# A planned attention stage: other times for its transfers, another spread of the projection products, and an order pinned into the convolution

## The chip, the cores and the metric

The kernel runs on one core of a Trainium2 chip. The metric is the device time of one execution in microseconds (us). The core has five engines with a queue of instructions each: TensorE (PE, with its weight loads listed as PEld), VectorE (DVE), ScalarE (ACT), GpSimd (POOL) and SyncE (SP), which here only issues DMAs.

## The reference

One layer of an encoder on 1024 tokens of width 1024, all in float32. A normed and modulated input goes through one projection whose columns feed a state-space group (SSD) and an attention group; their outputs are projected and added; a convolutional FFN and a final norm follow. Cut to what matters here:

```python
mod = (c_act @ w_ada[l] + b_ada[l])[:, None, :]          # six rows of 1024: shifts, scales, gates
h = rmsnorm(x, norm_mix_w[l]) * (1 + sc_m) + sh_m
z, xbc, dt_raw, q, k, v = jnp.split(h @ w_in[l], IN_SPLITS, axis=-1)
y_ssd = ssd_mixer(z, xbc, dt_raw, ...)   # begins with silu(causal_dwconv(xbc, conv_w) + conv_b), width 4
y_att = chunk_attention(q, k, v, rel_bias[l])   # 8 heads x 64, own chunk of 64 and the 8 before it
x = x + g_m * (jnp.concatenate([y_ssd, y_att], axis=-1) @ w_out[l])
h = rmsnorm(x, norm_ffn_w[l]) * (1 + sc_f) + sh_f
x = x + g_f * conv_ffn(h, w_up[l], ffn_conv_w[l], w_down[l])
return rmsnorm(x, final_norm_w)
```

## The kernel before

Every large product is made of three: both operands are split into a high part (fp32r) and the rest, and high x high, low x high and high x low are added in PSUM (`mm3`, lines 299 to 302). The stages follow each other on the one core: norm and first projection, attention (about 88 to 283 us of the trace), convolution and SSD with the output projection, FFN up, FFN down. The change lies in the attention and the start of the convolution.

**The attention** works on four pairs of heads p, eight query blocks i of 128 rows, and the two heads h of a pair. Each step has a letter: S scores (PE, into a PSUM tile `s`), X adds the bias table and takes the row maximum (DVE, into `p`), E exponential (ACT), R reciprocal of the row sum (DVE), N scaling (POOL), T transposition of a bank of probabilities (PE, into `tp`), H and L the split of that bank into `pt` (ACT copies the high half, DVE subtracts), W the product with the values (PE, into `pv`), C and Y the copy of half of it and its addition into `ya` (ACT, DVE). There is one `pv` bank, so the next W waits until Y has read the last one. B loads a bias table (issued by SP, for pair 0 by ACT) and M masks its corners (two memsets on POOL).

Into the gaps of this chain go the **projection products** F: sixteen groups of 24 products of 512 columns for the pairs 2 and 3, and for blocks 4 and 6 of the convolution's input (p = 4 and 5 in the plan). Their weights come by ld (DMA), wh (ACT, high half) and wl (POOL, low half). The high halves have two buffers in turn, and so do the low halves. Seven more steps, mload and m, load 512 KB of W_ada and take the row sums with the activated condition on DVE; each fills one column of `modc`.

**What sets the order.** `attention_plan` lists all these steps with an engine, a length in ns, what they depend on, a priority, and for transfers the earliest time `at` and how long they take. `Plan.run` places them one after the other, as a simulation with one clock for each engine would, and gives back their names by start time. The instructions are then issued in that order, and `InOrder` pins the order on each of PE, DVE, ACT and POOL: every instruction is tied behind the one before it on its engine. The transfers themselves are not pinned: their times in the table only decide where the steps that use them stand, and a scheduler orders the SP queue. A pinned engine waits at a step whose transfer is late, with everything behind it. `FP` (line 137) gives the priority of the n-th projection product by linear pieces, and with it how the 384 products are spread. `WIDE` stretches the lengths on DVE and ACT. With `slack`, a step that is ready within so many ns may be taken before the earliest one, by priority. The plan walks a Python set, so equal steps can fall differently from one build to the next; the orders shown below are of one build whose order on PE is the one in the trace of before.

Behind the plan, `e.on = False` ends the pinning, and the scheduler alone orders the **convolution**. `conv_silu(ft, dst)` makes one block: weights by `wu_pair` (DMA, ACT high, DVE low), 48 products (`gemm_ft`), an ACT scaling, three DVE multiply-adds, two ACT Silu. Block 4 takes its products from the rows that the plan left, block 6 from a PSUM tile `s` that the plan filled; blocks 5, 7 and 0 to 3 make their own. The code's order is 4, 6, 5, 7. `conv_mods` makes three more row sums behind each block.

Of the kernel before, what the change touches and what calls it, by code (L numbers as in the profile page):

```python
# [17 lines left out]
D = 1024  # L18
# [47 lines left out]
class Plan:  # L66


    TAIL = {"PE": 210, "V": 140, "A": 140, "G": 160, "D": 50}
    WIDE = 1.02  # L70
    OVER = {"PE": 0, "V": 80, "A": 100, "G": 60}

    def __init__(self, start, slack):
# [7 lines left out]
    def add(self, name, eng, ns, deps=(), prio=0, ring=None, until=None, result=0, at=0):  # L81
        self.tasks[name] = (eng, ns * self.WIDE if eng in "VA" else ns, tuple(deps), prio, ring, until, result, at)

# [50 lines left out]

CH2 = [(0, 0), (1, 0), (0, 1), (1, 1), (2, 0), (2, 1)]
CH3 = [(0, 0), (0, 1), (1, 0), (2, 0), (1, 1), (2, 1)]
FP = [(0, 0), (53, 4.04), (137, 7.71), (230, 9.78), (266, 11.49), (323, 14.11), (384, 24.63)]


def weighted_banks(u):  # L140
# [12 lines left out]
    return banks  # L153


def attention_plan(start=88300, slack=30, ahead=(1.14, 0.4)):
    pl = Plan({"PE": start, "V": start, "A": start, "G": start - 3000}, slack)
    for name, n in (("s", 2), ("p", 8), ("tp", 2), ("pt", 3), ("pv", 1), ("acc", 1), ("wh", 2)):
        pl.ring(name, n)
# [2 lines left out]
    V = {128: 300, 256: 420, 384: 560, 512: 690, 640: 810}  # L162
    A = {128: 410, 256: 510, 384: 620, 512: 730, 640: 830}
    G = {128: 380, 256: 480, 384: 580, 512: 690, 640: 800}
# [3 lines left out]
    def fprio(n):  # L168
        for (n0, s0), (n1, s1) in zip(FP, FP[1:]):
            if n <= n1:  # L170
                return s0 + (s1 - s0) * (n - n0) / (n1 - n0)
# [3 lines left out]
    for n, c in enumerate(chain):  # L175
        p, which, hh = c
        for j in range(24):
            deps = [prev] if prev else []
# [30 lines left out]
    for n, (p, which) in enumerate(ws):  # L209
        rel = ("FE", p, which, 1)  # L210
        deps = [("wl",) + ws[n - 2]] if n > 1 else []
        if n > 0:
            deps.append(("wh",) + ws[n - 1])
        at = 88000
# [5 lines left out]
    for p in range(4):  # L220
        for h in range(2):
            n = 2 * p + h
            if p:
                deps = [("X", (n - 3) // 2, 7, (n - 3) % 2)] if n >= 3 else []
                pl.add(("B", p, h), "D", 3600, deps, at=95000)
                pl.add(("M", p, h), "G", 330, [("B", p, h)], 4 * p)
            else:
                pl.add(("B", p, h), "D", 0, at=91800)
                pl.add(("M", p, h), "G", 330, [("B", p, h)], 4 * p)
        for i in range(8):  # L230
            n = 128 * min(i + 1, 5)
            u = 4 * p + i // 2
            for h in range(2):
                deps = []
                if p >= 2:
                    deps = [("MV", p, 0, 0), ("MV", p, 1, 0)]
                    if i > 3:
                        deps += [("MV", p, 0, 1), ("MV", p, 1, 1)]
                if (p, i) != (0, 0):
                    pl.add(("S", p, i, h), "PE", 2 * (n + 32) / 2.4 if n <= 512 else 587, deps,  # L240
                       u - ahead[0] + .1 * (i % 2) + .01 * h, "s", ("X", p, i, h),
                       at=(88000 if i < 4 else 91000) if p == 0 else 98000 if p == 1 else 0)
                else:
                    pl.add(("S", p, i, h), "D", 0, [], 0, "s", ("X", p, i, h))
                pl.add(("X", p, i, h), "V", V[n], [("S", p, i, h)] + ([("M", p, h)] if (p or i > 2) else [])
                       + ([("FA", p, 2, i // 4)] if p > 1 and i in (2, 6) else []),
                       u - ahead[1] + .1 * (i % 2) + .01 * h, "p", ("PF", p, i, h))
                pl.add(("E", p, i, h), "A", A[n], [("X", p, i, h)], u - ahead[1] + .1 * (i % 2) + .01 * h, result=100)
                pl.add(("R", p, i, h), "V", 150, [("E", p, i, h)], u - 2)
                pl.add(("N", p, i, h), "G", G[n], [("R", p, i, h)], u)  # L250
        for u in range(4):
            i0, i1 = 2 * u, 2 * u + 1
            banks = weighted_banks(u)
            for h in range(2):
                pr = 4 * p + u + .03 * h
                for t, bank in enumerate(banks):
                    w = sum(b[2] for b in bank)
                    a = (p, u, h, t)
                    deps = [("N", p, i0, h), ("N", p, i1, h)]
                    deps += turn  # L260
                    if p > 1 and u in (0, 2) and h + t == 0:
                        deps.append(("VT", p, 2, u // 2))
                    turn = [("T",) + a]
                    last = t == len(banks) - 1
                    pl.add(("T",) + a, "PE", w / 128 * 92.5, deps, pr + .01 * t, "tp", ("L",) + a)
                    pl.add(("H",) + a, "A", H[w], [("T",) + a], pr + .01 * t, "pt", ("W",) + a)
                    pl.add(("L",) + a, "V", L[w], [("H",) + a], pr + .01 * t)
                    deps = [("L",) + a] + ([("W", p, u, h, t - 1)] if t else [])
                    if p >= 2:
                        deps.append(("VL", p, 2, 0))  # L270
                        if u > 1:
                            deps.append(("VL", p, 2, 1))
                    pl.add(("W",) + a, "PE", sum(2 * (b[2] + 32) / 2.4 for b in bank), deps, pr + .01 * t - .005,
                           "pv" if t == 0 else None, ("Y", p, u, h))
                pl.add(("C", p, u, h), "A", 390, [("W",) + a], pr - .1)
                pl.add(("Y", p, u, h), "V", 410, [("C", p, u, h)], pr - .1)
                for i in (i0, i1):
                    pl.add(("PF", p, i, h), "D", 0, [("T",) + a])

    for n in range(7):  # L280
        deps = [("m", n - 2)] if n in (2, 3) else [("X", 2, 7, 0), ("X", 2, 7, 1)] if n > 3 else []
        pl.add(("mload", n), "D", 6000 if n < 4 else 5000, deps, at=92000)
        pl.add(("m", n), "V", 1220, [("mload", n)], 90)
    return pl

# [4 lines left out]
def tile_block(ctx: ExitStack, tc: tile.TileContext, x, ccol, pk, w_ada, w_first, w_ft, w_z,  # L290
               w_out, w_up, w_down, bias, fnw, xt, out, dbg=None):
    nc = tc.nc
    V, A, T, G = (InOrder(tc, e) for e in (nc.vector, nc.scalar, nc.tensor, nc.gpsimd))
# [79 lines left out]
    def wu_pair(src, hieng, loeng):  # L373
        t = raw_tile()
        nc.sync.dma_start(t, src)
        wh = wu.tile([P, 1024], F32R, tag="wh", name="wh")
        if not wls:
            wls.append(wu.tile([P, 2, 1024], F32R, tag="w2", bufs=1, name="wl"))
        wl = wls[0][:, rawc[0] % 2, :]
        split(wh, wl, t, hieng, loeng)  # L380
        return wh, wl
# [306 lines left out]
    for hh in range(2):  # L688
# [13 lines left out]
        for kt in range(KT):  # L702
            if hh == 0:
                if kt == 0:
                    bm = mods_first()
                else:
                    at = last_lo.ins if kt == 1 else bm.ins
# [164 lines left out]
    def conv_silu(ft, dst):  # L872
        if ft == 4:
            ps = rowb
        else:
            if ft == 6:
                ps = early["s"]
            else:
                wh, wl = wu_pair(w_ft[ft], A, V)
                ps = s_tile()  # L880
                gemm_ft(wh, wl, [ps[:, 0:512], ps[:, 512:1024]])
        w = [pkt[:, SCW + 4 * ft + j:SCW + 4 * ft + j + 1] for j in range(4)]
        A.activation(dst, ps, AF.Identity, scale=w[3], bias=pkt[:, SCB + ft:SCB + ft + 1])
        for j in range(1, 4):
            last = V.scalar_tensor_tensor(dst[:, j:S], ps[:, 0:S - j], w[3 - j], dst[:, j:S],
                                          op0=ALU.mult, op1=ALU.add)
        for hh in range(2):
            c = slice(hh * 512, hh * 512 + 512)
            sil[:] = [A.activation(dst[:, c], dst[:, c], AF.Silu).ins, last.ins]
        return last.ins  # L890
# [157 lines left out]
    for k in attention_plan().run():  # L1048
        if k[0] in ops:
            ops[k[0]](*k[1:])  # L1050
    for e in (T, V, A, G):
        e.on = False
    es_at.close()


# [33 lines left out]
    def conv_mods(n, at):  # L1089
        for _ in range(CMODS[n]):  # L1090
            k = wosc[0]
            wosc[0] += 1
            t = xs[:, 2 * (k % 4):2 * (k % 4) + 2, :].rearrange("p a b -> p (a b)") if n < 5 else wos[:, k % 3, :]
            mod_col(todo.pop(0), t, at)
# [8 lines left out]
    conv_mods(0, last_v[0])  # L1103
    for g in range(2):
        conv_mods(2 * g + 1, conv_silu(4 + g, bt_[g]))
        if g == 1:
            V.tensor_tensor(gcol[:, 0:8], modc[:, G_M:G_M + 8], gbias[0], ALU.add)
            cols_to_dram(gcol[:, 0:8], tp_tile()[0:8, 0:P], th512()[0:8, 0:P], gmd)
            for t, k in ((rowb[:, 0:512], 0), (gm1, 4)):
                nc.sync.dma_start(t.rearrange("p (a b) -> p a b", a=4), rows_from(gmd, k, 4))  # L1110
        conv_mods(2 * g + 2, conv_silu(6 + g, ct_[g]))
# [394 lines left out]
    at = None  # L1506
    for c in range(NT):
# [5 lines left out]
        if c == 1:  # L1513
            at = wout_rhs(0, 1)
# [6 lines left out]
        n, k = ((0, slice(0, 3)), (2, slice(0, 4)), (3, slice(0, 3)))[c] if c < 3 else (c + 1, slice(0, 3))  # L1521
# [715 lines left out]
```

## Time and profile before

| what | value |
|---|---|
| median of 3 runs | 1163.94 us (1162.77 to 1166.97) |
| profiled execution | 1162.48 us, its span 1160.8 us |
| granted TensorE clock | 0.998 |
| PE, PEld busy | 1143.3 us (98%), 971.4 us (84%) |
| DVE, ACT, POOL busy | 79%, 51%, 13% of the span |
| DMA | 170.72 MB, mean 147 GB/s |

The span runs from the first to the last instruction of the profiled execution; times in the views count from its start. The prediction's rows come from the list of waits (who waited for whom: total, times, longest), from busy times by stretch, and from the timeline of one engine. A row of the timeline has the start and the duration in us, the engine, the line of the kernel, the operation with what it writes and reads, the shapes and, in brackets, the idle time of the engine before it with the instruction that ended it. Line 60 is the helper of `InOrder`, so all pinned instructions carry it; they are told apart by their tiles. A matmul's end is modelled, and successive ones overlap. Rows that follow each other are merged (x8).

### The profile page before, as it was taken

How to read it: one execution, taken by the hardware profiler on the slowest of the kernel's cores; microseconds unless marked ns; L12 is line 12 of the kernel's file. 1: busy time of each engine (PE TensorE's matmuls, PEld its weight loads, DVE VectorE, ACT ScalarE, POOL GpSimd, SP SyncE). 2: the span in 40 equal slices, each digit the busy share in tenths (PEclk: the TensorE clock that was granted, in tenths of full speed). 3: DMA queues.
4: the chain of work that ended last, by engine and by line, in shares of the span. 5: the costliest groups of instructions: out<-in, count | busy, mean ns of one | idle time of the engine just before them, and what ended most of it. 6: DMA issues, size and time to landing. Idle time of an engine off the chain costs nothing.

```text
span 1160.8 us, 15796 instructions
## 1 busy us (share of the span) xinstructions
PE 1143.3 (98%) x5833; PEld 971.4 (84%) x5833; DVE 913.4 (79%) x1365; ACT 592.6 (51%) x987; POOL 149.7 (13%) x180
## 2 busy tenths in 40 slices
PE   9998999999999999999999999999999999999997
PEld 8887988887889988887788888888888888888886
DVE  7857765676875788469999998889888869666987
ACT  5746665564345765576543445334533444433445
POOL 1104333230000455100000000000000000000522
PEclk9999999999999999999999999999999999999999
DMA  9967323335466532231223322332223378633444
GB/s 333 368 168 207 70 68 96 108 109 182 148 215 238 219 109 74 87 113 55 109 84 134 136 82 82 109 136 82 85 106 118 121 288 301 241 119 126 155 145 155
DMA packets 68189, 170.72 MB, mean 147 GB/s; under 512 B 6976, under 2 KB 11792, under 8 KB 66704
## 3 DMA queue, kind: packets, MB, share of 16 engines
q1 hardware_dynamic: 60624, 144.42, 37.4%
q10 hardware_dynamic: 7488, 25.30, 5.5%
q8 instruction: 46, 0.75, 0.3%
q14 instruction: 31, 0.25, 0.1%
HBM read 127.44 MB, written 32.81 MB: 138 GB/s over the span
## 4 chain that ended last, share of the span: by engine, by line
PE 84%; DVE 10%; DMA 2%; ACT 1%; issue 1%; SPq 0%; POOL 0%; POOLq 0%; DVEq 0%; ACTq 0%
PE acc L60 6%; PE wops L1256 5%; PE dn L302 5%; PE dn L301 5%; PE dn L300 5%; PE uY L302 5%; PE uY L301 5%; PE uY L300 5%; PE s L60 4%; PE uX L302 3%; PE uZ L301 3%; PE uZ L300 3%; PE uZ L302 3%; PE uX L301 3%; PE uX L300 3%; PE pv L60 2%
## 5 line engine op out<-in xcount | busy, mean ns | idle before, releaser
L301 PE MATMUL dn<-w 128*128 128x512 f32 x292 | 105.9, 389 | 0.4 <-DVE w L311 0.4
L300 PE MATMUL dn<-w 128*128 128x512 f32 x292 | 105.8, 389 | 0.0
L302 PE MATMUL dn<-w 128*128 128x512 f32 x292 | 98.1, 389 | 0.0
L302 PE MATMUL uY<-tH,w 128*128 128x512 f32 x248 | 96.5, 389 | 0.0
L300 PE MATMUL uY<-tH,w 128*128 128x512 f32 x248 | 96.5, 389 | 0.0
L301 PE MATMUL uY<-tL,w 128*128 128x512 f32 x248 | 96.5, 389 | 0.0
L2027 POOL TENSOR_TENSOR ya<-ya,xs 128x512 f32<-128x512 f32 x4 | 14.7, 3692 | 551.0 <-ACT xs L2023 551.0
L310 ACT ACTIVATE w<-ya 128x1024 fp32r<-128x1024 f32 (+1 forms) x41 | 39.1, 954 | 85.2 <-PE uY L302 75.2
L1256 PE MATMUL wops<-hH,yhl 128*128 128x512 f32 x224 | 72.8, 397 | 0.6 <-DVE yhl L311 0.6
L301 PEld LDWEIGHTS dn<-w 128*128 128x128 f32 x292 | 54.8, 188 | 12.2 <-DVE w L311 0.8
L302 PEld LDWEIGHTS dn<-w 128*128 128x128 f32 x292 | 54.7, 188 | 11.8 <-DVE w L311 0.4
L300 PEld LDWEIGHTS dn<-w 128*128 128x128 f32 x292 | 54.8, 188 | 11.3
L60 POOL TENSOR_SCALAR p<-p,st 128x640 f32<-128x640 f32 (+4 forms) x64 | 43.5, 686 | 119.1 <-DVE st L60 96.0
L310 ACT ACTIVATE w<-xs 128x1024 fp32r<-128x1024 f32 (+1 forms) x41 | 39.1, 954 | 37.0 <-PE uY L302 31.1
L300 PEld LDWEIGHTS uY<-tH,w 128*128 128x128 f32 x248 | 46.6, 188 | 9.7
L302 PEld LDWEIGHTS uY<-tH,w 128*128 128x128 f32 x248 | 46.5, 188 | 9.7
L301 PEld LDWEIGHTS uY<-tL,w 128*128 128x128 f32 x248 | 46.5, 188 | 9.6
L60 DVE CUSTOM_DVE_ANT_0 p<-s,bias 128x640 f32<-128x640 f32 (+4 forms) x58 | 38.1, 674 | 19.0 <-PE s L60 17.0
L1679 DVE SCALAR_TENSOR_TENSOR a<-cv,pkt,a 128x1023 f32<-128x1023 f32 (+1 forms) x40 | 51.0, 1277 | 0.1
L60 ACT ACTIVATE p<-p,st 128x640 f32<-128x640 f32 (+4 forms) x64 | 44.1, 692 | 13.3 <-DVE st L60 13.1
L60 DVE TENSOR_TENSOR pt<-tp,pt 128x512 fp32r<-128x512 f32 (+2 forms) x72 | 41.8, 595 | 11.1 <-ACT pt L60 10.6
L1679 DVE SCALAR_TENSOR_TENSOR a<-cg,pkt,a 128x1023 f32<-128x1023 f32 (+1 forms) x40 | 49.7, 1278 | 0.0
(527 smaller groups left out, 3332.7 us busy)
## 6 DMA issues: line engine op xcount, KB each, us to landing
gz<-a ACTq DMA_DIRECT2D x10, 1024.0 KB, 5.1
ya<-in_w_up_dram SPq DMA_DIRECT2D x11, 768.0 KB, 4.1
xs<-in_w_up_dram SPq DMA_DIRECT2D x11, 768.0 KB, 4.3
adat<-in_w_ada_dram SPq DMA_DIRECT2D x14, 512.0 KB, 5.3
raws<-in_w_ft_dram SPq DMA_DIRECT2D x14, 512.0 KB, 3.6
qk<-qk SPq DMA_DIRECT2D x56, 128.0 KB, 2.4
xs<-in_w_ada_dram SPq DMA_DIRECT2D x12, 512.0 KB, 4.7
gy<-a ACTq DMA_DIRECT2D x10, 512.0 KB, 2.6
```

What stands on the lines that cost most here:

```text
L60: i = op(*a, **k)
L300: T.matmul(ps, lh, rh, start=start, stop=False, skip_group_check=more)
L301: T.matmul(ps, lh, rl, start=False, stop=False, skip_group_check=more)
L302: T.matmul(ps, ll, rh, start=False, stop=stop, skip_group_check=more)
L310: i = A.activation(hi, src, AF.Copy) if ehi is A else ehi.tensor_copy(hi, src)
L1256: i = op(*a, **k)
L1679: V.scalar_tensor_tensor(a[:, j:S], c[:, 0:S - j], w[2 - j], a[:, j:S], op0=ALU.mult, op1=ALU.add)
L2027: G.tensor_tensor(src, src, fnr[:, halves[1]], ALU.mult)
```

## The change

Four things change. The plan's times of transfers: the bias tables of pair 0 at 92.0 and 93.9 us instead of both at 91.8, the first four loads of W_ada from 98.5 us and 8 or 7 us long instead of from 92.0 and 6, the other three 9 us long instead of 5. The planner's settings: lengths on DVE and ACT stretched by 1.04 instead of 1.02, and no slack instead of 30 ns. The knots of `FP`. And where the pinning ends: for POOL behind the plan as before, for DVE and ACT behind block 4 of the convolution with its three row sums, for PE behind the products of block 5.

```diff
-    WIDE = 1.02
+    WIDE = 1.04
...
-FP = [(0, 0), (53, 4.04), (137, 7.71), (230, 9.78), (266, 11.49), (323, 14.11), (384, 24.63)]
+FP = [(0, 0), (53, 3.74), (138, 7.31), (228, 10.09), (270, 10.64), (324, 14.74), (384, 23.55)]
...
-def attention_plan(start=88300, slack=30, ahead=(1.14, 0.4)):
+def attention_plan(start=88300, slack=0, ahead=(1.14, 0.4)):
...
-                pl.add(("B", p, h), "D", 0, at=91800)
+                pl.add(("B", p, h), "D", 0, at=92000 + 1900 * h)
...
-        pl.add(("mload", n), "D", 6000 if n < 4 else 5000, deps, at=92000)
+        pl.add(("mload", n), "D", 8000 if n < 2 else 7000 if n < 4 else 9000, deps, at=98500)
         pl.add(("m", n), "V", 1220, [("mload", n)], 90)
...
     for k in attention_plan().run():
         if k[0] in ops:
             ops[k[0]](*k[1:])
-    for e in (T, V, A, G):
-        e.on = False
+    G.on = False
     es_at.close()
...
     for g in range(2):
         conv_mods(2 * g + 1, conv_silu(4 + g, bt_[g]))
+        for e in (T,) if g else (V, A):
+            e.on = False
```

DVE at the first row sum m(0) of W_ada, before. `ISA ya,modc` is the sum over a load that lies in `ya`, `ISA p` an X with its bias table, `pt<-tp,pt` an L, `ya<-pv,tl` a Y, RECIPROCAL an R:

```order
L60 RECIPROCAL st_72<-st_72 128x1
L60 TENSOR_TENSOR pt<-tp,pt 128x512
L60 TENSOR_TENSOR ya<-pv,tl 64x2x128
L60 TENSOR_TENSOR pt<-tp,pt 128x384
L60 RECIPROCAL st_72<-st_72 128x1
L60 ISA ya,modc<-ya,rows 128x8x128
L60 ISA modc 128x1
L60 RECIPROCAL st_72<-st_72 128x1
L60 TENSOR_TENSOR pt<-tp,pt 128x512
L60 TENSOR_TENSOR ya<-pv,tl 64x2x128
```

DVE at the same sum now:

```order
L60 TENSOR_TENSOR pt<-tp,pt 128x384
L60 ISA p,st_72<-s,bias 128x640
L60 ISA st_72 128x1
L60 RECIPROCAL st_72<-st_72 128x1
L60 ISA p,st_72<-s,bias 128x640
L60 ISA st_72 128x1
L60 TENSOR_TENSOR pt<-tp,pt 128x512
L60 TENSOR_TENSOR ya<-pv,tl 64x2x128
L60 TENSOR_TENSOR pt<-tp,pt 128x512
L60 ISA ya,modc<-ya,rows 128x8x128
L60 ISA modc 128x1
```

The sum has moved 16 places down DVE's queue, from between query blocks 5 and 6 to behind block 7 of pair 0 and the first two subtractions of the third pair of blocks.

DVE at the first of the three late sums, whose loads lie in `qk`, before:

```order
L60 TENSOR_TENSOR pt<-tp,pt 128x512 x2
L60 RECIPROCAL st_72<-st_72 128x1
L60 ISA p,st_72<-s,bias 128x640
L60 ISA st_72 128x1
L60 RECIPROCAL st_72<-st_72 128x1 x2
L60 TENSOR_TENSOR pt<-tp,pt 128x256
L60 TENSOR_TENSOR pt<-tp,pt 128x512
L60 ISA qk,modc<-qk,rows 128x1024
L60 ISA modc 128x1
L60 TENSOR_TENSOR ya<-pv,tl 64x2x128
```

And now:

```order
L60 TENSOR_TENSOR pt<-tp,pt 128x256
L60 TENSOR_TENSOR ya<-pv,tl 64x2x128
L60 ISA p,st_72<-s,bias 128x128
L60 ISA st_72 128x1
L60 ISA p,st_72<-s,bias 128x128
L60 ISA st_72 128x1
L60 ISA p,st_72<-s,bias 128x256
L60 ISA st_72 128x1
L60 TENSOR_TENSOR pt<-tp,pt 128x512 x2
L60 RECIPROCAL st_72<-st_72 128x1 x2
L60 ISA qk,modc<-qk,rows 128x1024
L60 ISA modc 128x1
```

It has moved from right behind pair 2's last bias addition and two subtractions to behind the first three bias additions of pair 3.

PE at the end of block 6's products, which the plan places, before (`s_2852` is block 6's tile, `wh` and `wl_948` the two halves of the weights, `s_3126` block 7's tile):

```order
L60 MATMUL s_2852<-hH1_85,wl_948 128x512
L60 MATMUL s_2852<-hH1_85,wh_2615 128x512
L60 MATMUL s_2852<-hL1_87,wh_2615 128x512
L60 MATMUL s_2852<-hH1_85,wl_948 128x512
L300 MATMUL s_3126<-hH0_84,wh_3123 128x512
L301 MATMUL s_3126<-hL0_86,wh_3123 128x512
L302 MATMUL s_3126<-hH0_84,wl_948 128x512
```

PE there now (`s_2877` is block 6's tile, `s_3053` block 5's):

```order
L60 MATMUL s_2877<-hH1_85,wl_948 128x512
L60 MATMUL s_2877<-hH1_85,wh_2611 128x512
L60 MATMUL s_2877<-hL1_87,wh_2611 128x512
L60 MATMUL s_2877<-hH1_85,wl_948 128x512
L60 MATMUL s_3053<-hH0_84,wh_3050 128x512
L60 MATMUL s_3053<-hL0_86,wh_3050 128x512
L60 MATMUL s_3053<-hH0_84,wl_948 128x512
```

The 48 products of block 5 stood before among the attention's last transpositions and weighted products, ahead of this place; now all of them stand behind block 6's, and block 7 follows them. On SP the bias table of pair 1 now stands ahead of the first two loads of W_ada, which stood before and behind a move of pair 1's keys.

## The prediction, as put on record

> **What bounds the kernel now.** I read the page's busy line first (busy time, share of the span, instructions).
>
> ```profile
> PE 1143.3 (98%) x5833; PEld 971.4 (84%) x5833; DVE 913.4 (79%) x1365; ACT 592.6 (51%) x987; POOL 149.7 (13%) x180
> ```
>
> TensorE (PE) has work for 98% of the span. No instruction of arithmetic goes away in this change, so all that it can win is PE's idle time: 1160.8 - 1143.3 = 17.5 us. The list of waits of PE says which part of that lies where the change works (total, times, longest):
>
> ```profile
> PE pv L60 <- DVE ya L60: 3.8, 2, 2.1
> PE s L302 <- DVE wl L311: 0.9, 1, 0.9
> PE tp L60 <- DVE st L60: 0.9, 1, 0.9
> ```
>
> All four waits are in the attention and at the start of the convolution. Busy time by stretch (PE, PEld, DVE, ACT, POOL, then granted clock, DMA share, GB/s) places three of them: PE is whole in most stretches (20.00) and short in three.
>
> ```profile
> 88.00:100.00 12.00, 11.14 (x68) 9.36 (x67) 9.44 (x39) 9.37 (x27) 5.48 (x13) 1.00 0.89 232
> 100.00:120.00 20.00, 17.94 (x122) 16.17 (x120) 16.63 (x46) 12.51 (x30) 7.96 (x14) 1.00 0.61 166
> 120.00:140.00 20.00, 20.00 (x137) 18.42 (x137) 15.71 (x45) 15.21 (x38) 6.47 (x9) 1.00 0.28 60
> 180.00:200.00 20.00, 20.00 (x118) 17.83 (x118) 11.26 (x29) 10.72 (x23) 6.36 (x6) 1.00 0.33 81
> 200.00:220.00 20.00, 18.26 (x119) 16.11 (x118) 11.82 (x35) 9.65 (x26) 4.23 (x9) 1.00 0.39 122
> ```
>
> The timeline of PE shows the four holes (start, duration, what; in brackets the idle time and who ended it):
>
> ```profile
> 92.54 0.49 PE L60 MATMUL tp<-ident,p 128*128 128x128 f32 x3
> 93.11 0.27 PE L60 MATMUL tp<-ident,p 128*128 128x128 f32 x1
> 94.24 0.44 PE L60 MATMUL tp<-ident,p 128*128 128x128 f32 x2 [0.86 <-DVE st L60]
> 103.23 1.34 PE L60 MATMUL s<-qk 128*128 128x320 f32 x8
> 106.63 1.15 PE L60 MATMUL pv<-pt,v 128*128 128x256 f32 x8 [2.06 <-DVE ya L60]
> 209.00 0.40 PE L60 MATMUL acc<-hH,wl 128*128 128x512 f32 x1
> 211.14 0.75 PE L60 MATMUL pv<-pt,v 128*128 128x256 f32 x4 [1.74 <-DVE ya L60]
> 283.56 0.39 PE L300 MATMUL s<-hH,wh 128*128 128x512 f32 x1
> 283.78 0.39 PE L301 MATMUL s<-hL,wh 128*128 128x512 f32 x1
> 285.11 0.50 PE L302 MATMUL s<-hH,wl 128*128 128x512 f32 x1 [0.94 <-DVE wl L311]
> ```
>
> Products overlap, so the idle time in brackets understates a hole. I measure from start to start and take off what the row before needs when nothing is late. A 512-column product needs 0.227 (283.56 to 283.78), though it is shown as 0.39: its end overlaps the next by 0.16. A transposition needs 0.11 (three in 0.49, one in 0.27), the eight products at 103.23 need 1.34 - 0.16 = 1.18. The holes are 1.13 - 0.11 = **1.02**, 3.40 - 1.18 = **2.22**, 2.14 - 0.23 = **1.91** and 1.33 - 0.23 = **1.10**: together **6.25 us**.
>
> Whether loading weights says the same: PEld's busy time falls to 16.17 between 100 and 120 against 18.42 in the next stretch (2.25 less), and to 16.11 between 200 and 220 against 17.83 before (1.72 less). [...]
>
> **The change part by part.**
>
> *Loads of W_ada (holes 2 and 3).* DVE stands in a pinned order, and a row sum m waits there for its load:
>
> ```profile
> 104.36 1.23 DVE L60 CUSTOM_DVE_ANT_0 ya<-ya,rows 128x1024 f32<-128x1024 f32 x1 [2.73 <-DMA ya<-in_w_ada_dram]
> 111.77 1.28 DVE L60 TENSOR_TENSOR pt<-tp,pt 128x512 fp32r<-128x512 f32 x2
> 200.68 0.80 DVE L60 CUSTOM_DVE_ANT_0 p<-s,bias 128x640 f32<-128x640 f32 x1
> 209.52 1.23 DVE L60 CUSTOM_DVE_ANT_0 qk<-qk,rows 128x1024 f32<-128x1024 f32 x1 [2.73 <-DMA qk<-in_w_ada_dram]
> ```
>
> The addition ya that frees PE's only pv bank is queued behind m (in the order above, the fourth row after the first m): that is how 2.73 us of DVE become 2.22 and 1.91 of PE. The table had counted on the first load at 92.0 + 6.0 = 98.0; it came at 104.36. Now it counts on 98.5 + 8.0 = 106.5. The late three were counted at 5.0 after the last bias addition of pair 2; that ended at 200.68 + 0.80 = 201.48 and the sum began 8.04 later; now 9.0 are allowed. Both allowances exceed what was traced, by 2.1 and 1.0. On DVE m(0) now stands behind the two subtractions that began at 111.77. They ended at 113.05; less the two holes before them (3.24), and less another row sum (1.23) that no longer stands ahead, m(0) comes due at 108.6 to 109.8. The issues decide when the loads land:
>
> ```profile
> 96.37 0.65 SPq L1034 DMA_DIRECT2D ya<-in_w_ada_dram  x1
> 97.13 1.25 SPq L455 DMA_DIRECT2D qk<-qk  x1
> 98.43 0.59 SPq L1034 DMA_DIRECT2D ya<-in_w_ada_dram  x1
> 99.12 0.86 SPq L958 DMA_DIRECT2D bias<-in_bias_dram  x1
> 202.57 1.29 SPq L1037 DMA_DIRECT2D qk<-in_w_ada_dram  x3
> ```
>
> Now the bias table of pair 1 goes first, in the place of 96.37, and both loads follow the move at 97.13, at about 98.4 and 99.0. From the second issue to the sum it took 104.36 - 98.43 = 5.9, so 104.9: 3.7 ahead of need. I take off both holes whole, **-4.1**. Kept for the range: none of it, should a load still be late.
>
> *The first two bias tables (hole 1) and the one of pair 1.* POOL works in a pinned order too (the last row is PE's):
>
> ```profile
> 91.67 0.34 POOL L60 MEMSET bias<- 64x64 f32 x2
> 93.27 0.34 POOL L60 MEMSET bias<- 64x64 f32 x2 [1.25 <-DMA qk<-qk]
> 93.71 1.60 POOL L60 TENSOR_SCALAR p<-p,st 128x256 f32<-128x256 f32 x3
> 98.38 0.80 POOL L60 TENSOR_SCALAR p<-p,st 128x640 f32<-128x640 f32 x1 [0.36 <-PE tp L60]
> 105.19 0.34 POOL L60 MEMSET bias<- 64x64 f32 x2 [6.01 <-DMA bias<-in_bias_dram]
> 109.53 1.03 PE L60 MATMUL tp<-ident,p 128*128 128x128 f32 x8
> ```
>
> The scaling that the transposition at 94.24 needs (the first of the three from 93.71; DVE, which the trace names there, had been done) is queued behind the memset at 93.27, which waits for the second table. With 92.0 and 93.9 in place of twice 91.8 the scaling stands ahead of it: **-1.0**. The price lies at the third memset: it now stands ahead of the scalings of blocks 4, and they wait for its table. Issued at 96.4 instead of 99.12, with the 6.07 that it took before (105.19 - 99.12), that table lands at 102.4; memset 0.34 and three scalings of 0.80 end at 105.2. The first transposition that needs the third is the one at 109.53; less the two holes ahead of it (3.24) it comes due at 106.3. The margin is 1.1 us, so a new wait of 0 to 2: I take **+0.3**.
>
> *The end of the attention (hole 4).* DVE writes the low half of the next weights only after the last product that reads the same half:
>
> ```profile
> 283.82 2.36 DVE L311 TENSOR_TENSOR wl<-raws,wh 128x1024 fp32r<-128x1024 f32 x2 [5.26 <-PE s L60]
> 272.92 0.39 PE L60 MATMUL s<-hL,wh 128*128 128x512 f32 x1
> 273.40 0.33 PE L60 MATMUL tp<-ident,p 128*128 128x128 f32 x1
> 271.33 0.58 ACT L60 ACTIVATE pt<-tp 128x512 fp32r<-128x512 f32 x1
> ```
>
> Before, the 48 products of block 5 had been spent inside the attention, and the block that follows needs this half at once. With PE pinned, they stand behind the last product of block 6: 48 x 0.227 = 10.9 us of cover for 1.2 us of DVE. **-1.1**. DVE and ACT now do no convolution between the attention's last halves, so the small hole at 272.92 (0.48 - 0.23 = 0.25) should close: **-0.25**. The pinning costs that filler: between a transposition and its weighted product lie an ACT copy (0.58), a DVE subtraction (0.64) and handovers, about 1.7. In the new order 1.6 to 2.5 us of other PE rows stand there, so **+0.2**, with bounds of 0 and, with no cover for ten banks, 17.
>
> *At nothing:* slack 0, the cushion 1.04 and the new spread change only places. PE changes its kind of work 253 times instead of 255 in this part, so the gaps at each change stay.
>
> Sum: -1.0 - 4.1 - 1.1 - 0.25 + 0.3 + 0.2 = **-5.95**, say -6.0. The profiled execution took 1162.48 (span 1160.8, 1.7 around it), so 1156.5; the median of the runs is 1.46 higher, 1163.94, and I forecast **1157.9**. What follows stands in the same order on every engine, so the gain should be carried to the end.
>
> **Rivals.**
>
> *A: a transfer still decides.* More bytes now stand ahead of the first loads:
>
> ```profile
> ya<-in_w_ada_dram SPq DMA_DIRECT2D x4, 512.0 KB, 4.2
> bias<-in_bias_dram SPq DMA_DIRECT2D x6, 320.0 KB, 4.6
> ```
>
> With weights, table, move, both loads and the next weights sharing, 2.5 MB at the 232 GB/s of the stretch end at 95.7 + 10.8 = 106.5; or the memset holds POOL 2 us longer. One such wait of 2 to 3 us comes back: gain 2 to 5, about 1160.4. For it: margins of 1.0 and 1.1; against it: those of 2.1 and 3.7. Chance 0.22. [...]
>
> *B: slower, the uncovered tail.* If ACT or DVE lags, each of the ten last banks shows its chain of 1.7: +17 with no cover. It turns the gain into a loss once more than 6 us show, that is when the cover per bank averages below 1.1. At 0.5 per bank: +12 - 6 = +6, 1170. Against it: the order keeps 1.6 or more. Chance 0.06.
>
> *C: the change doesn't do what it says.* The times in the table only order instructions; if PE waits for another engine at the same places, nothing comes of it: 1163.9. DVE's 79% speak against it. Chance 0.04.
>
> *D: more.* The added waits stay out and the wider cushion shortens some of the gaps at PE's changes of work too: gain 7.5 to 9, about 1155.7. Chance 0.06.
>
> **How the numbers follow.** The forecast, a gain of 5.0 to 7.5, has 0.62. A measurement of this kernel can tell about 0.5% from no change, here 5.8 us: 0.44 of the 0.62 lie beyond it and 0.18 within. Faster 0.44 + 0.06 = 0.50; same 0.18 + 0.22 + 0.04 = 0.44; slower 0.06. The range 1155.0 to 1161.5 leaves out B, C and the far ends of A and D.
>
> **What would show it.** In the profile after: the two waits of pv for ya and the one of s for wl gone from PE's list; DVE's sums m without a DMA behind them; PE whole between 100 and 120 and between 200 and 220; block 5's products behind block 6's. Wrong if POOL waits long for a bias table with PE behind it, if PE waits for pt or ya after 240, or if the attention ends less than 4 us earlier.

## The result, and the profile after

The changed kernel takes 1154.31 us (median of 5 runs, 1153.49 to 1155.25) against 1163.89 for the kernel before (5 runs, 1162.77 to 1166.97): ratio 0.9915, interval 0.9900 to 0.9931. It is 9.6 us faster where 6.0 were forecast, and 0.7 below the lower end of the range. The profiled execution took 1154.31, its span is 1152.6: 8.2 less than before.

PE's list of waits after the change (first and last rows):

```profile
PE warm L60 <- POOL mhalf L352: 1.6, 1, 1.6
PE xps L60 <- ACT ya L60: 0.9, 1, 0.9
PE uX L302 <- DVE w L311: 0.6, 1, 0.6
...
PE vps L60 <- DVE hL L544: 0.2, 1, 0.2
```

None of the four waits named in the prediction is left; what is left lies outside the attention. The busy times by stretch, in the columns of before:

```profile
88.00:100.00 12.00, 12.00 (x73) 10.65 (x72) 9.79 (x38) 9.26 (x28) 4.78 (x12) 1.00 0.88 238
100.00:120.00 20.00, 20.00 (x140) 18.55 (x140) 18.13 (x51) 15.00 (x38) 8.80 (x17) 1.00 0.73 179
200.00:220.00 20.00, 20.00 (x125) 17.70 (x124) 13.01 (x35) 10.24 (x26) 7.07 (x7) 1.00 0.43 128
```

PE is whole in all three, and loading weights rose from 16.17 to 18.55 and from 16.11 to 17.70. At the place of the largest hole (PE, start and duration) the scores are now followed without a break, and on DVE the first sum of either group begins with nothing in brackets, so it waits for no transfer:

```profile
103.84 1.33 PE L60 MATMUL s<-qk 128*128 128x320 f32 x8
105.01 0.39 PE L60 MATMUL acc<-hL,wh 128*128 128x512 f32 x1
```
```profile
108.83 1.22 DVE L60 CUSTOM_DVE_ANT_0 ya<-ya,rows 128x1024 f32<-128x1024 f32 x1
208.24 1.20 DVE L60 CUSTOM_DVE_ANT_0 qk<-qk,rows 128x1024 f32<-128x1024 f32 x1
267.35 1.23 DVE L311 TENSOR_TENSOR wl<-raws,wh 128x1024 fp32r<-128x1024 f32 x1 [0.49 <-ACT wh L310]
```

The last row is the low half of the next weights: it is written at 267.35, while block 5's products run, and PE does not wait for it.

POOL around the bias tables of pair 0 and pair 1:

```profile
93.24 0.35 POOL L60 MEMSET bias<- 64x64 f32 x2 [0.25 <-DMA bias<-in_bias_dram]
93.68 0.59 POOL L60 TENSOR_SCALAR p<-p,st 128x384 f32<-128x384 f32 x1
...
100.81 0.35 POOL L60 MEMSET bias<- 64x64 f32 x2 [2.13 <-PE s L60]
101.26 3.93 POOL L60 TENSOR_SCALAR p<-p,st 128x640 f32<-128x640 f32 x5
```

Pair 1's table was issued at 95.90 and its memset ran at 100.81, 4.9 later and not the 6.07 of the forecast; five scalings follow at once and PE waits for none of them.

All holes of PE over 0.11 us from 87 to 345, measured from start to start, were 6.96 in sum before and are 0.35 now. The part as a whole is 7.5 shorter, so gaps under 0.11 us lost another 0.9; 0.7 went outside this part (0.2 ahead of it, 0.5 behind).

One thing must be known for the numbers below. The planner walks through a Python set, and candidates that are equal to it (two loads with the same time, say) come out in an order that differs from one build to the next. The changed program that ran is of another build than the one listed above; the rows shown are the same in both. The kernel before, built anew for the experiments, took 1159.34 to 1159.76 and not 1163.89. So all experiments carry a fixed rank for equal candidates, and are compared with d_before and d_after, which have the traced orders. By the intervals of the ratios a median carries about 1.0 to 1.6 us.

### The profile page after: what moved, and what is told of

It reads as the page before. It is cut to its first block, busy times and chain, and to the rows that moved or that the text cites. A ratio compares the mean times of both kernels' runs of the same rounds, so it can differ in the third digit from the quotient of the medians.

```text
span 1152.6 us, 15803 instructions
## 1 busy us (share of the span) xinstructions
PE 1141.3 (99%) x5833; PEld 971.8 (84%) x5833; DVE 913.7 (79%) x1365; ACT 592.6 (51%) x987; POOL 156.1 (14%) x180
## 4 chain that ended last, share of the span: by engine, by line
PE 89%; DVE 7%; ACT 1%; DMA 1%; issue 1%; POOL 0%; POOLq 0%; DVEq 0%; ACTq 0%
PE acc L60 8%; PE wops L1257 6%; PE dn L302 6%; PE dn L300 6%; PE dn L301 6%; PE s L60 5%; PE uY L302 5%; PE uY L301 5%; PE uY L300 5%; PE uX L302 3%; PE uZ L301 3%; PE uZ L302 3%; PE uZ L300 3%; PE uX L301 3%; PE uX L300 3%; PE pv L60 3%
## 5 line engine op out<-in xcount | busy, mean ns | idle before, releaser
L302 PE MATMUL dn<-w 128*128 128x512 f32 x292 | 98.3, 390 | 0.0
L302 PE MATMUL uY<-tH,w 128*128 128x512 f32 x248 | 96.5, 389 | 0.0
L2028 POOL TENSOR_TENSOR ya<-ya,xs 128x512 f32<-128x512 f32 x4 | 18.2, 4588 | 551.1 <-ACT xs L2024 551.1
L302 PEld LDWEIGHTS dn<-w 128*128 128x128 f32 x292 | 54.7, 188 | 12.1 <-DVE w L311 0.8
L60 POOL TENSOR_SCALAR p<-p,st 128x640 f32<-128x640 f32 (+4 forms) x64 | 46.5, 734 | 116.4 <-DVE st L60 104.1
L302 PEld LDWEIGHTS uY<-tH,w 128*128 128x128 f32 x248 | 46.5, 188 | 9.6
L1257 PEld LDWEIGHTS wops<-hH,yhl 128*128 128x128 f32 x224 | 41.9, 188 | 9.5 <-DVE yhl L311 1.3
```

What stands on the lines that cost most here:

```text
L60: i = op(*a, **k)
L302: T.matmul(ps, ll, rh, start=False, stop=stop, skip_group_check=more)
L1257: i = op(*a, **k)
L2028: G.tensor_tensor(src, src, fnr[:, halves[1]], ALU.mult)
```

## The experiments

**A first try at the rank.** The edit, in the planner (shown with the rank that d_before has; c_before, c_sums and c_pin have "10" in place of "437", and c_after takes the reverse of the order in which the steps are listed):

```
+        def tie(k):
+            return hashlib.md5(("437" + repr(k)).encode()).digest()
-            for k in open_:
+            for k in sorted(open_, key=tie):
```

Four kernels had ranks that gave TensorE's order of the traced kernels, but turned round the two weight loads (2,2) and (3,0), and here and there other equal steps. The low halves of the two weights take each other's buffer, so these kernels compute other projections than the reference.

> The kernel before, with one thing added: equal candidates of the planner are taken by a fixed rank, chosen so that TensorE's order is that of the traced kernel before. Theory (the traced program stands for the kernel, and its profiled execution of 1162.48 lay 1.4 below the median because waits for transfers vary from run to run): ratio 1.000, that is 1163 to 1165; the four holes of 1.0, 2.2, 1.9 and 1.1 us on TensorE again; runs spread over 2 us or more. Rival (the runs of before differ because its builds differ in order): runs within 1 us of each other, at a median more than 1 us away from that of before.

Measured 1169.54.

> The changed kernel with the same kind of fixed rank, chosen so that TensorE's order is that of the traced changed kernel. Theory: ratio 0.991 to 0.992, 1154 to 1155, runs within 2 us since no wait for a transfer is left on TensorE. Rival (part of the gain is a lucky build): 1156 to 1158.

Measured 1161.05. The row that carries it, from c_after's waits of PE:

```profile
PE acc L60 <- POOL wl L60: 4.2, 2, 2.1
```

Neither expectation can be judged: the turned loads alone add waits for the low half of the weights. The two others, c_sums (1162.09) and c_pin (1167.59), were run with the same fault:

> Before in its traced order, with nothing but the seven row sums of W_ada put later in that order (the first four 8 places or more, the late three 2 or more), and of the loads only the third and fourth, which can only follow the first and second sum. Theory (the sums stood ahead of their transfers): holes 2 and 3 go, 4.1 us; the planner's own costs show 0.5 to 0.7 us of new idle time at 118 to 122, where VectorE is full; gain 3.4 to 3.6, about 1160.4, ratio 0.997; holes 1 and 4 stay at 1.0 and 1.1. Rival (the wait of VectorE only passes on to what is queued behind, and the other spread of the products is what removed it): gain under 1.

> Before in its traced order, with nothing but the pinned order carried on into the convolution. The prediction's terms: hole 4, 1.1, and the small hole of 0.25 go, 0.2 comes back: gain 1.15, 1162.8, ratio 0.999. Theory after the result (all three small holes behind 272 go, 0.69, and nothing comes back): gain 1.8 to 2.3, 1161.6 to 1162.1, ratio 0.998. Rival (the uncovered tail): slower by 2 or more.

They are taken up again below with a rank that keeps the order of these loads. What they leave is a price: c_after took 6.2 us more than d_after (1154.88, below). Its trace has two new holes on PE, both in this wait and of 2.26 each, and behind one of them the granted clock was 0.50 (136.99 to 140.40; the last section has the rows). Its rank turns round row sums too, but no hole stands at them.

**The traced orders.** d_before and d_after: the same edit with the rank "437" and "36".

> The kernel before with a fixed rank for equal candidates, chosen so that the order on all engines, that of the weight loads, of the bias tables and of the loads of W_ada included, is that of the traced kernel before. Theory (the order decides the time, the chip and the build otherwise don't): 1163 to 1165 and the four holes of 1.0, 2.2, 1.9 and 1.1 us on TensorE, wherever the kernel before, built anew, comes out. Rival (this chip is faster): at the time of the kernel before as built here, 1159 to 1160.

> The changed kernel with such a rank, in the order of the traced changed kernel on all engines. Theory: 1154 to 1155, 9 to 10 below the one before in its traced order. Rival (this chip is faster): 1150 to 1151.

1164.01 and 1154.88, beside 1159.34 for the kernel before built anew on that chip. The theory holds: the order makes the time, not the chip. The profiled execution of d_before is one of 1164.22, and shows what the trace of before (1162.48) did not. PE at hole 2, then the busy times by stretch (the first of the last three columns is the granted clock):

```profile
108.16 1.16 PE L60 MATMUL pv<-pt,v 128*128 128x256 f32 x8 [2.97 <-DVE ya L60]
...
109.79 2.33 PE L60 MATMUL s<-qk 128*128 128x320 f32 x8
```
```profile
108.00:109.40 1.40, 1.24 (x9) 1.24 (x10) 1.40 (x5) 0.06 (x1) 1.40 (x2) 1.00 0.31 90
109.40:112.10 2.70, 2.70 (x11) 2.56 (x10) 2.64 (x8) 2.05 (x5) 0.17 (x2) 0.52 0.49 148
```

The hole is 3.1 here instead of 2.2, and behind it the granted clock is 0.52 for a while: the eight products with 320 columns take 2.33 instead of 1.33, and with their neighbours about 1.2 us go. Hole 1 is 1.6 instead of 1.0, hole 3 only 1.0. These waits end with transfers and differ from run to run.

**One part alone on before.** The steps of the plan are moved by hand:

```
+    steps = attention_plan().run()
+    for k, anchor in (...):
+        steps.remove(k)
+        steps.insert(steps.index(anchor) + 1, k)
```

A pair names a step and the one that it is put behind. d_sums:

```
+            (("m", 3), ("L", 0, 3, 0, 2)), (("m", 2), ("L", 0, 3, 0, 1)),
+            (("m", 1), ("Y", 0, 2, 0)), (("mload", 3), ("m", 1)),
+            (("m", 0), ("L", 0, 2, 0, 1)), (("mload", 2), ("m", 0)),
+            (("m", 4), ("L", 2, 2, 1, 1)), (("m", 6), ("X", 3, 0, 1)), (("m", 5), ("L", 2, 3, 0, 2)),
```

> Before in its traced order with nothing but the seven row sums of W_ada later in that order, and with them the third and fourth load. Theory: holes 2 and 3 go, 4.1 us, and 0.5 to 0.7 us of new idle time shows at 118 to 122, where VectorE is full: 3.4 to 3.6 below before in its traced order; holes 1 and 4 stay. Rival (the wait only passes on to what is queued behind): less than 1 below it.

1160.18, 3.8 below d_before: the theory. PE where DVE is full:

```profile
123.96 0.48 PE L60 MATMUL acc<-hL,wh 128*128 128x512 f32 x1
124.51 0.50 PE L60 MATMUL s<-qk 128*128 128x512 f32 x1
```

0.55 from start to start where 0.23 would do: 0.32 of the foreseen 0.5 to 0.7. Holes 2 and 3 are gone, 1 and 4 are there. Hole 1 is 2.39 in this execution, and a new hole of 0.74 begins at 89.4; both lie ahead of all that was moved. So 3.8 is the difference of the medians, and these holes don't add up to it.

d_pin, the change's last two pieces alone:

```
-    for e in (T, V, A, G):
-        e.on = False
+    G.on = False
...
+        for e in (T,) if g else (V, A):
+            e.on = False
```

> Before in its traced order with nothing but the pinned order carried on into the convolution. The prediction's terms: 1.1 + 0.25 - 0.2 = 1.15 below before in its traced order. Theory after the result (the three small holes behind 272 go whole, 0.69, and nothing comes back): 1.8 to 2.3 below it. Rival (the uncovered tail): 2 or more above it.

1162.53, 1.5 below d_before, which the runs' width doesn't tell from 1.15, from 1.8 or from nothing. Its trace does: hole 4 and the holes at 272.92 and 273.57 are closed, and one is new.

```profile
257.35 0.22 PE L60 MATMUL pv<-pt,v 128*128 128x128 f32 x1
257.95 0.55 PE L60 MATMUL pv<-pt,v 128*128 128x128 f32 x3 [0.37 <-DVE pt L60]
```

In the old spread the pinned tail lets 0.53 us of its chains show.

e_swap only turns equal loads round:

```
+            (("mload", 1), ("mload", 0)),
+            (("mload", 6), ("mload", 4)), (("mload", 5), ("mload", 6)),
```

> Before in its traced order, with nothing changed but which of equal loads of W_ada is issued first: now the one that is summed first. In the traced order the first sum reads the second of two loads, issued 2.06 later (96.37 and 98.43), and the first of the late three reads the second of three, 0.4 later. Theory (the sum waits for that one transfer): hole 2 shrinks by 2.06 to 0.2 to 1.1, hole 3 by 0.4, and a slowed clock behind hole 2 goes where it was: 2.4 to 3.7 below before in its traced order, 1160.3 to 1161.6. Rival (the loads share the transfer engines and land together): less than 0.7 below it.

1159.92, 4.1 below d_before, even a little more than the theory's most. The first two sums that wait, on DVE:

```profile
101.48 1.23 DVE L60 CUSTOM_DVE_ANT_0 ya<-ya,rows 128x1024 f32<-128x1024 f32 x1 [0.69 <-DMA ya<-in_w_ada_dram]
...
205.31 1.23 DVE L60 CUSTOM_DVE_ANT_0 qk<-qk,rows 128x1024 f32<-128x1024 f32 x1 [0.66 <-DMA qk<-in_w_ada_dram]
```

0.69 and 0.66 instead of 2.73 and 2.73, with the sums at their old places (this execution took 1158.24, 1.7 below the median). PE has 0.2 left of hole 2 and nothing of hole 3, and a new hole of 0.7 at 106.7. Holes 2 and 3 were there because the first sum of either group reads a load that was not issued first. The time is that of the kernel before built anew (ratio 1.0000, 0.9991 to 1.0008); whether that build has the loads in this order is not shown.

e_bias, the second memset two scalings later:

```
+            (("M", 0, 1), ("N", 0, 2, 0)),
```

> Before in its traced order, with the memset of the second bias table put behind the next two scalings on GpSimd, and nothing else. Theory: hole 1 goes (1.0 in the one traced execution, 1.6 in the other) and 0.2 comes back, since the bias addition that needs that table is later: 0.8 to 1.4 below before in its traced order. Rival (the transposition waits for something else at the same time): less than 0.4.

1162.70, 1.3 below d_before by the medians, within their width. The trace says that the hole only moved, from the transpositions to the scores:

```profile
93.01 0.75 PE L60 MATMUL s<-qk 128*128 128x320 f32 x4
95.03 0.71 PE L60 MATMUL s<-qk 128*128 128x320 f32 x3 [1.27 <-DVE st L60]
```

The second table itself is late. DVE's bias addition waits for its memset, and with it the bank that these scores need:

```profile
94.27 0.69 DVE L60 CUSTOM_DVE_ANT_0 p<-s,bias 128x512 f32<-128x512 f32 x1 [2.01 <-POOL bias L60]
```

So the transposition did wait for the memset, as the theory says, but 1.3 came back where the theory allowed 0.2. The time tells neither from the rival.

**The parts together.** e_all has the moves of d_sums, d_pin and e_bias, with the old table FP, cushion and slack.

> Before in its traced order with all three of these moves: the sums later, the second memset later, the pinned order carried on; the table of the spread, the cushion and the slack as before. Theory (the parts add up: 3.8 and 1.5 as measured, 1.2 for the memset): 6.5 below before in its traced order, 1157.5; what is missing to the changed kernel's 1154.9, some 2.6, is what the new spread is worth. Rival (the new spread is worth only the 0.7 that the planner's costs show at 118 to 122): 1155.6.

1157.26, 6.75 below d_before (theory 6.5). 2.4 to the changed kernel are left. Two holes of its profiled execution (1158.28, the slowest of its eleven), on PE:

```profile
95.30 0.87 PE L60 MATMUL s<-qk 128*128 128x320 f32 x4 [1.01 <-DMA qk<-qk]
...
108.59 0.66 PE L60 MATMUL tp<-ident,p 128*128 128x128 f32 x4 [1.06 <-POOL p L60]
```

The first is that of e_bias (1.2; the trace names another of several releasers). In the changed kernel three projection products instead of one stand ahead of the first scores of block 4, and four of them and a weighted product instead of nothing between these and the second, so the late table costs nothing there. That is read from the new spread; no run undoes the spread alone. The second is the scaling behind pair 1's table.

f_table adds to e_all that this table, B(1,0), goes ahead of the loads; f_after_table takes the changed kernel and puts it behind them:

```
+            (("B", 1, 0), ("M", 0, 0)),
...
+            (("B", 1, 0), ("mload", 0)),
```

> The kernel with the three moves (sums later, second memset later, pinned order carried on) and one more: the bias table of pair 1 issued ahead of the first two loads of W_ada instead of behind them. In the profile without this TensorE waits 1.23 us at 107.26 for a scaling that is queued on GpSimd behind that table's memset. Theory (the table's early issue, which the prediction booked as a price of 0.3, is a gain once the wait ahead of it is gone): 0.7 to 1.3 below the 1157.3 of the three moves. Rival (the scaling is late for another reason): less than 0.4 below.

> The changed kernel in its traced order, with the bias table of pair 1 issued behind the first two loads of W_ada, as before the change. Theory: the memset on GpSimd comes 2 later, five scalings are queued behind it, and TensorE waits 0.7 to 1.3 near 107: 1155.6 to 1156.2. Rival (there is slack behind the memset in the new order): less than 0.4 above the changed kernel's 1154.9.

f_table took 1156.88: the hole at 107 is gone from its trace, but 0.4 by the medians is less than the width, and at the edge of the rival's range. From the other side it is clear: f_after_table took 1158.11, 3.2 above d_after, more than expected. POOL there, and PE's first wait:

```profile
105.19 0.35 POOL L60 MEMSET bias<- 64x64 f32 x2 [6.71 <-DVE pt L60]
105.63 4.68 POOL L60 TENSOR_SCALAR p<-p,st 128x640 f32<-128x640 f32 x6
```
```profile
PE tp L60 <- POOL p L60: 2.0, 2, 1.2
```

The memset runs at 105.19 instead of 100.81 (the trace puts POOL's idle time down to DVE). Its runs spread from 1156.79 to 1161.29, those of d_after from 1153.75 to 1155.88: with a wait for a transfer on PE's path the spread is back. The profiled execution was the fastest, 1.9 above d_after. The two runs with a granted clock of 0.999 took 1156.79 and 1156.81, the three with 0.996 took 1160.64 to 1161.29: most of what exceeds the expectation goes with a lowered clock.

**The changed kernel with one part undone.** e_unpin is the diff of d_pin undone.

> The changed kernel in its traced order, with the pinned order ended behind the plan as before. Theory (the pin is worth the holes at the end of the attention, 1.1 and 0.7): 1.5 to 1.8 above the changed kernel, 1156.4 to 1156.7. Rival (in the new order the same holes would not open): less than 0.5 above it.

1155.22, 0.3 above d_after: the rival. In the new order the same wait is smaller:

```profile
PE s L304 <- DVE wl L313: 0.4, 1, 0.4
```

(L304 and L313 are L302 and L311 of the kernel before.) The hole is 0.58 instead of 1.10.

f_early puts the first sum alone back:

```
+            (("m", 0), ("R", 0, 5, 0)),
```

> The changed kernel in its traced order, with the first row sum of W_ada alone put back to the place it had before the change, behind the reciprocal of block 5. Theory (the place of the sum is what costs): VectorE stands there until the second load lands near 103.5, TensorE gets a hole of 2 to 3, and where the hole is near 3 the granted clock falls to half for some us behind it, 1.2 more: 1156.8 to 1159.2. Rival (the issue of the loads, not the place of the sum, was the point): less than 0.5 above the changed kernel's 1154.9.

1160.60, 5.7 above d_after: the theory's mechanism, at more than its price. DVE, then PE and its clock:

```profile
105.61 1.23 DVE L60 CUSTOM_DVE_ANT_0 ya<-ya,rows 128x1024 f32<-128x1024 f32 x1 [4.49 <-DMA ya<-in_w_ada_dram]
```
```profile
103.37 0.39 PE L60 MATMUL acc<-hH,wh 128*128 128x512 f32 x1
107.65 2.50 PE L60 MATMUL s<-qk 128*128 128x320 f32 x8 [3.89 <-DVE st L60]
```
```profile
107.00:110.00 3.00, 2.35 (x9) 2.35 (x10) 2.22 (x8) 2.26 (x6) 1.08 (x2) 0.51 0.48 137
110.00:113.80 3.80, 3.80 (x19) 3.67 (x19) 3.13 (x9) 1.80 (x5) 1.33 (x2) 0.50 0.39 120
```

The load lands at 105.61, so the hole is 4.05, and the halved clock lasts from 107.0 to 113.9. In the changed kernel's own trace this load was issued at 97.61 and landed at 105.02; its sum begins at 108.83, 3.8 later, where the prediction had 3.7.

f_tail takes the tail's cover away:

```
+    steps = attention_plan().run()
+    tail = [k for k in steps[steps.index(("T", 3, 2, 0, 0)):] if k[:2] in (("F", 4), ("F", 5), ("FE", 4))]
+    for k in [k for k in steps if k not in tail] + tail:
```

> The changed kernel in its traced order, with the 32 products of the blocks 4 and 5 that stand among the last ten banks of the attention put behind its last product, and the copy that follows block 4's with them. This takes the prediction's cover away on purpose. Rival B of the prediction as it was priced: up to 17 slower with no cover. Theory (an idle TensorE can lose no more than the work that filled the gaps, 32 x 0.227 = 7.3): 4 to 7.3 slower, 1159 to 1162.

1159.35, 4.5 above d_after: the theory, and far from 17. PE's waits there:

```profile
PE pv L60 <- DVE pt L60: 1.1, 2, 0.7
...
PE tp L60 <- DVE pt L60: 0.7, 2, 0.4
```

## Why the prediction was wrong: the right mechanisms, and a sum that was too small

**What failed.** Two steps of the sum. First, 5.95 were added up for the profiled execution and 8.2 came. Of the 2.2 between them about 0.5 are costs that did not come, 0.2 small holes that were not counted, 0.9 gaps under 0.11 us and 0.7 lie outside the part that changes. The spread, the cushion and the slack had been put "at nothing"; without them and without the earlier issue of pair 1's table (e_all) 2.4 of the gain is missing. Second, the median was set 1.46 above the profiled execution, and it lies on it. The two together are the 3.6 that the forecast missed.

**Right.** The four holes and their causes: all closed, 6.25 forecast and 6.25 gone in the profiled execution. The small hole at 272.92 too; with it went those at 273.57 and 275.51 (0.13 and 0.31; 0.16 of the last kind is left), which were not counted. For hole 1 the cure took more than the prediction says: with the second memset moved and the old spread (e_bias, e_all) 1.2 to 1.4 comes back at the scores.

**The costs that did not come.** "The margin is 1.1 us, so a new wait of 0 to 2: I take +0.3." Nothing was waited for, and the sign was wrong: the earlier issue of pair 1's table is a gain. It hid behind holes 1 and 2, and shows as soon as they are closed (1.2 in e_all's trace, 3.2 in f_after_table). The step that failed is that the first transposition's need, 109.53 less the holes, was set against the new memset only; against the old one, at 105.19, with three scalings behind it that end at 107.9, a need at 106.3 would have been missed by 1.6. "The pinning costs that filler ... +0.2": 0.53 with the old spread (d_pin); with the new one no gap over 0.11 is left there but the 0.16 just named, which was 0.31 before, so the cost did not come.

**The gaps that were not in the sum.** 0.9 in gaps under 0.11 us, and 0.7 outside the part that the change touches. What shortened them is not shown: no run changes the cushion, the slack or `FP` alone.

**The offset.** "The median of the runs is 1.46 higher, 1163.94, and I forecast 1157.9" carried the distance between one execution and the median over to the changed kernel. It was no constant: it was made of the same waits. Before, they end with transfers, and the profiled execution had short ones (2.2 and no slowed clock; 3.1 and 1.2 of slowed clock in d_before's). After, there are none, and median and profiled execution are both 1154.31. With that step alone set right the forecast would have been 1156.5, 2.2 from the result, and the range, moved by as much, would have held it.

**Hole 4 and the pin.** Its place and size were right, but "-1.1" is its worth in the old order. In the new one the rest of the change had done most of that work: 0.3 (e_unpin, within the runs' width).

**The loads.** "The issues decide when the loads land": so they do. The landing foreseen at 104.9 came at 105.02, but by luck: the load was issued 1.4 earlier than foreseen and took 7.4 instead of 5.9. And the prediction took for granted that the sums read them in the order of issue, though it saw that the first sum came 5.9 behind the second issue. e_swap shows that this alone is behind holes 2 and 3 (4.1 by the medians). The change cured it by moving the sums (d_sums, 3.8); the first sum of the changed kernel still reads the load that is issued second (f_early). Against the kernel before as built anew, the changed kernel gains only 4.5 (d_after, ratio 0.9962, 0.9950 to 0.9975). How the changed kernel's time varies when it is built anew without a rank is not shown.

**The rivals.** A (a transfer still decides) and C did not come. B's price was wrong as such: the work that covered the waits comes to 7.3, and f_tail, without that cover, measured 4.5. D (gain 7.5 to 9) was the nearest and still too small; added waits stayed out and short gaps shrank as it said, though that the cushion did it is not shown. A chance of 0.06 was too little: terms that are left out because they can only gain belong into the range.

**Open.** How the 2.4 between e_all and the changed kernel divide: its trace shows 1.2 at the late second table, 1.2 at pair 1's table, 0.5 at the tail and 0.3 at 123, together more than the 2.4. Of these only pair 1's table was measured by itself in the changed kernel, and the two measurements (0.4 and 3.2) differ.

## What to carry to other kernels

When a wait ends with a transfer, look first at which of the issued transfers it reads, and issue them in the order of use: that was worth as much here as moving the consumer (4.1 in e_swap, 3.8 in d_sums). A profiled execution with such waits is one draw (hole 2 was 2.2 in before and 3.1 in d_before); price them from several, and don't carry its distance to the median over to a kernel that no longer waits. A step that stands behind a hole can be late too (the scaling behind pair 1's table, 1.2 in e_all): ask of each step that moves earlier whether it would have been the next to wait.

## What the hardware showed beside that

At some of PE's holes the granted clock fell to half for a while. Behind the 3.1 of d_before it was 0.52 from 109.40 to 112.10 and 0.90 from there to 116.00; the share lost in the two stretches is that of about 3.4 us at half. At the 4.05 of f_early it was 0.51 from 107.00 to 110.00, 0.50 to 113.80 and 0.99 to 116.00, which makes about 6.8 us, twice as long; the drop began about 0.6 before that hole ended. Behind the 2.2 of before it was 1.00 in the whole stretch from 100 to 120. The length of the hole alone does not decide: c_after has two equal ones of 2.26, and the clock fell at the first and stayed whole at the second (busy time by stretch, PE first; the first two rows are those of the first hole):

```profile
133.58:136.99 3.41, 1.36 (x6) 1.14 (x7) 0.79 (x4) 1.26 (x4) 3.41 (x3) 1.00 0.20 44
136.99:140.40 3.41, 3.41 (x15) 3.31 (x14) 1.61 (x5) 0.92 (x2) 0.15 (x1) 0.50 0.39 148
171.12:174.53 3.41, 2.00 (x13) 1.45 (x11) 1.54 (x6) 2.59 (x7) 2.30 (x2) 1.00 0.00 0
174.53:177.94 3.41, 2.72 (x12) 2.22 (x13) 0.00 (x0) 0.00 (x0) 1.20 (x2) 1.00 0.42 139
```

What decides is not shown. So the hole of 3.1 in d_before cost its length and, behind it, about 1.2 to the halved clock; the one of 2.2 in before cost its length alone.
